# Rotating the weight rings of a decoder layer from group to group, two homes for its decay tables, and reloads paced by weight splits

## The chip, the cores and the metric

The kernel runs on one core of one Trainium2 chip. The metric is device time in microseconds of one execution; the number given for a kernel is the median of its runs. A profiled execution is shown by its span, from the first to the last instruction.

The engines are named as the profile names them: PE is TensorE (its weight loads are PEld), DVE is VectorE, ACT is ScalarE, POOL is GpSimd, and SP is the engine whose queue issues nearly all transfers. POOL's queue issues a few.

## The reference, cut to what matters

One hybrid decoder layer, batch 1, 512 tokens, model width 2048, everything in float32:

```python
h = rms_norm(x, g_mix);  z = h @ w_in            # 2048 x 7168: aq ak av | rq rk rv rg
a_out = moba_attention(rotary(norm(aq)), rotary(norm(ak)), av)      # 8 heads of 128
r = retention_chunkwise(rotary(rq), rotary(rk) * 128**-0.5, rv)     # 8 heads of 128
r = r * rsqrt(mean(r * r) + eps) * g_ret;  r_out = silu(rg) * r
x = x + concat(a_out, r_out) @ w_o               # 2048 x 2048
h2 = rms_norm(x, g_ffn)
x = x + (silu(h2 @ w_gate) * (h2 @ w_up)) @ w_down                  # 5632 wide
x = x + (p @ w_ple_proj) * sigmoid(rms_norm(x, g_ple) @ w_ple_gate + b)
```

In `retention_chunkwise` the scores of a chunk of 128 tokens are multiplied by a decay table, a power of one number per head: `decay[i, j] = g ** (i - j)` for `i >= j`, zero elsewhere. Head h has its own g, so each head needs its own table.

## The kernel before, in words

**Two parts for precision.** A float32 operand is used as a high part (a copy rounded to float32r, made by ACT) and a low part (the rest, made by DVE). `split` makes both. A product is three matmuls (`mm3`): high by high, high by low, low by high. A raw weight tile of 128 x 1024 is split by one ACT operation (`wh`, L54) and one DVE operation (`wl`, L55).

**Groups, parts, units and steps.** The large products run as groups (class `Group`). A group multiplies a 512-token operand by weights in blocks [kh, nh] of two by two, with seven products instead of eight (a scheme of Strassen's kind). The seven products are called parts, in the order 1, 5, 6, 3, 7, 2, 4. A group has four units (three in some down-projection groups), and a step is one part of one unit: 12 matmuls. So a whole group has 28 steps. Some groups run the first three parts in an order by units (`in_units`). For each step, the weight tile is added up two to three steps ahead on DVE (`add`, L83), split two steps ahead (`extract`), and multiplied (`multiply`).

**The raw tiles and their rings.** A group takes four blocks of each unit: "11", "12", "22" and "21". Each lies in a raw tile of 512 KB, in one of three rings of four tiles, with the tags `l1`, `bd` and `c`. Part 1 splits "11"; part 5 adds "12" to it, part 6 adds "22"; part 3 splits "22"; part 7 adds "22" to "12" and splits that, and then "21" is loaded into the ring of "22"; part 2 splits "21"; part 4 adds "21" to the tile of "11" and splits that. So the tile of "12" is done with at the split of part 7, that of "21" at the addition of part 4, and that of "11" at the split of part 4. As soon as a tile is done with, `load_next` loads a block of the next group into that ring:

```python
    elif p == "4":
        plus(r("11"), r("11"), r("21"))
        self.load_next("22", u)          # in add
    ...
    if p == "4":
        self.load_next("11", u)          # in extract
    elif p == "7":
        self.load_next("12", u)
```

Three groups (the first up/gate group, the last down-projection group and the first of the last gate) take sums that POOL's queue has formed ahead in DRAM (`sums`); their tiles are called by the part, "1", "5", "6" and so on, and use the same rings.

**The factors.** The other operand of a group is kept as one tile per part (`Factors`): `s_o` for w_o, `s_c` for the up/gate groups, `s_d` for the down projection. Factors are either written straight into their tile (`into`) or stored in DRAM (`spill`: a `mix`, `h` or `a` tensor) and loaded back: `back` for w_o, `reload` for the others. These reloads go through SP's queue, 512 KB to 1.5 MB each.

**Heads and slots.** The attention and retention heads run beside the projections that make their q and k. Time there is counted in slots (`tick`): a slot is six matmuls of a projection. The tables ATTEND, RETAIN, V_AT and MIXED say at which slot each piece of a head is put. For a retention head RETAIN holds: `begin`, `load` (its decay table, tile `dec`), four `scores` slots, two `normed` slots, `scaled` and `result`. `scores` multiplies the scores by the decay table (L1053) and splits the product. `normed` sums squares, takes their power on POOL (L86) and multiplies by the gate tile `sg`; `scaled` (L1089) applies the power; `result` transposes on TensorE. `mixed(i)` (at the slot MIXED[i]) makes the factors of two heads from their results: those of head groups 0 to 5 go to DRAM; for groups 6 and 7, parts 1, 5, 6 and 3 are written straight into `s_o`, and parts 7, 2 and 4 go to DRAM through the `o` tiles (four of them).

Slots 1 to 160 lie beside the projections; 161 to 176 beside p @ w_ple_proj (loop over n from 0 to 3, four slots each), whose results are copied by ACT into spare tiles (`pp`, L1192) and stored by POOL's queue; 177 to 192 beside the first eight steps of w_o's first group, two slots each (`take_over`).

**Order.** The program is written in one order, and a planner with a timing model orders each engine's instructions. `keep_in_program_order` pins some (the matmuls up to step 8 of w_o), `issue_after` puts one instruction behind another of the same engine, and `paced` makes a transfer wait until a given instruction is done. An engine, SP's queue included, runs its instructions in order. A tile of a ring or tag can't be written until its last reader is done. `lead` holds the last weight split.

Of the kernel before, what the change touches and what calls it, by code (L numbers as in the profile page):

```python
# [17 lines left out]
P = 128  # L18
T = 512
# [14 lines left out]
def layer_kernel(ctx, tc, x, xT, pT, g_mix, wqk, w_vg, qk_norm, g_ret, w_ow, g_ffn,  # L34
# [218 lines left out]
            k, n = (k - self.part) % 8, where.shape[1]  # L253
            return nc.sync.dma_start(self.tile(k // 6)[:, k % 6:k % 6 + n].bitcast(F32), where.bitcast(F32))

    def reload(tiles, where, n, wait={}, part=0):

        def go(p):
            tiles[p].load(part, where[p][:, :min(n, 6)])
            if n == 8:  # L260
                tiles[p].load(6, where[p][:, 6:])
            if n < 6 and p == "4":
                tiles[p].load(6, where[p][:, n:])
        def after(p):
            if not part:
                tiles[p] = Factors(p, 0, n != 6)
            later(wait[p], lambda: go(p)) if p in wait else go(p)
        return after
# [9 lines left out]
    class Group:  # L278
        def __init__(self, src, units, tiles, evac, order=None, after=lambda p: None, ready=lambda p, u: None, sums=None):
            self.sums = sums  # L280
            self.src, self.units, self.tiles, self.evac = src, units, tiles, evac
            self.after, self.ready = after, ready
            self.raw, self.bank, self.w, self.next = {}, {}, {}, None
            self.pinned = self.ends = self.spread = False
            self.left = {p: len(units) for p in ORDER}
            steps.extend((self, p, u) for p, u in
                         (order or [(p, u) for p in ORDER for u in range(len(units))]))

        def load(self, q, u):
            where = None  # L290
            tag = {"11": "l1", "12": "bd"}.get(q, "c")
            if self.sums:
                q = {"11": "1", "12": "5", "22": "6"}.get(q, q)
                tag = {"5": "bd", "7": "bd", "6": "c", "2": "c"}.get(q, "l1")
                where = self.sums[q][u] if q in self.sums else None
            a = SOURCE.get(q, q)
            t = rawq.tile([P, 2, T], F32, name="raw", tag=tag)
            ins = nc.sync.dma_start(t, self.src(int(a[0]) - 1, int(a[1]) - 1, self.units[u]) if where is None else where)
            if self.pinned:
                tc.keep_in_program_order(ins)  # L300
            self.raw[q, u] = t
# [8 lines left out]
        def add(self, p, u):  # L310
            r = lambda q: self.raw[q, u]
            if self.sums:
                return
            if p == "5":
                plus(r("11"), r("11"), r("12"))
            elif p == "6":
                plus(r("11"), r("11"), r("22"))
            elif p == "7":
                plus(r("12"), r("12"), r("22"))
                self.load("21", u)  # L320
            elif p == "4":
                plus(r("11"), r("11"), r("21"))
                self.load_next("22", u)

        def extract(self, p, u):
            wh = wq.tile([P, 2, T], F32R, name="wh", tag="wh")
            wl = wq.tile([P, 2, T], F32R, name="wl", tag="wl")
            with ExitStack() as queued:
                if first_parts:
                    queued.enter_context(tc.issue_after(first_parts.pop(0).ins))  # L330
                parts = split(wh, wl, self.raw[p if self.sums else SOURCE[p], u])
            lead[0] = parts[0]
            self.w[p, u] = wh, wl
            if self.sums and p in "1563":
                self.load({"1": "3", "5": "7", "6": "2", "3": "4"}[p], u)
            if self.sums and p == "2":
                self.load_next("22", u)
            if p == "4":
                self.load_next("11", u)
            elif p == "7":  # L340
                self.load_next("12", u)
            self.ready(p, u)
            return parts

# [33 lines left out]
                self.after(p)  # L378
                self.evac(self, p)

    def chained(groups):
        for a, b in zip(groups, groups[1:]):
            a.next = b
        for q in ("11", "12", "22"):
            for u in range(len(groups[0].units)):
                groups[0].load(q, u)
# [259 lines left out]

    kinds = [values(0), pairs(), values(1), gates()]
    groups = [Group(lambda kh, nh, u, j=j: w_vg[j, kh, nh, u], range(4), s_h, kinds[j]) for j in range(4)]
    for j in range(3):
        groups[j].next = groups[j + 1]  # L650
    groups[0].pinned = True
    def beside(i):

# [375 lines left out]
    def retain(qk, v, j, h):  # L1029
# [3 lines left out]
            own["qk"] = [x if isinstance(x, tuple) else parted(x) for x in (qk[j], qk[2 + j])]  # L1033

        def load():
            own["dec"] = ap.tile([P, P + T], F32, name="dec", tag="dec")
            nc.sync.dma_start(own["dec"], decay_c[h])

        def scores(kb):
            if kb == 0:  # L1040
                own["p"] = p_tiles()
                own["sg"] = rp_tile("sg", (P, NB, HD))
                nc.sync.dma_start(own["sg"], sgd[:, :, h * HD:(h + 1) * HD])
            PH, PL = own["p"]
            (qH, qL), (kH, kL) = own["qk"]
            q0 = min(kb, 2) * P
# [49 lines left out]
            nc.scalar.activation(a, tp, AF.Copy, scale=gr[:, h:h + 1])  # L1096
            return a

        return begin, load, scores, normed, scaled, result


    def back(p, pairs):
# [5 lines left out]
    def mixed(i, made):  # L1108
# [3 lines left out]
        with ExitStack() as queued:  # L1112
            for ins in lead if i < 2 * NPAIR - 1 else ():
# [7 lines left out]
              ((23, four(26, 31), four(31, 38), 44), (34, four(39, 45), four(45), 53)),  # L1121
              ((48, four(53), four(57), 70), (59, four(63, 73), four(72, 77), 81)),
              ((75, four(79), four(83), 92), (85, four(89), four(93, 103), 107)))
    RETAIN = (((104, 103, 108, 114, 118, 121), (112, 113, 116, 122, 126, 128)),
# [3 lines left out]
    MIXED = (37, 57, 83, 109, 139, 152, 179, 191)  # L1128

    def heads(i, made):  # L1130

# [15 lines left out]
                end(last, result)  # L1147
        else:
            for j, (first, at, step_s, step_n, step_x, last) in enumerate(RETAIN[i - NPAIR]):
                begin, load, scores, normed, scaled, result = retain(made, v, j, 2 * (i - NPAIR) + j)  # L1150
                plan.extend(((first, begin), (at, load), (step_x, scaled)))
                put(scores, *range(step_s, step_s + NB))
                put(normed, step_n, step_n + 1)
# [18 lines left out]
    for n in range(NS):  # L1172
        wh, wl = weights()
        accs = [acc_p.tile([P, T], F32, name="acc", tag="acc") for _ in range(NB)]
        for b in range(NB):
# [7 lines left out]
                t = ev_tile("t", 2, name="pp")  # L1183
            elif n == 1 and b < 2:
                if b == 0:
                    room = ap.tile([P, 2, T], F32, name="pp", tag="rope2")
                t = room[:, b]
            elif n:
                t = rm_tile("pp")
# [2 lines left out]
            copied = nc.scalar.activation(t, accs[b], AF.Copy)  # L1192
            copies.append(copied)
            nc.gpsimd.dma_start(ppd[b][:, n], t)
        for p in "156" if n < 3 else ():
            paced(back(p, slice(2 * n, 2 * n + 2)), copied)
    paced(back("3", slice(0, 6)), copied)
    first_parts.append(copies[4 * NS - 5])
    acc_ctx.close()

# [3 lines left out]
    def take_over(i):  # L1204

        if 0 <= i < 8:
            tick()
            tick()
        if i == 5:
            at_ctx.close()  # L1210
            pools["chainY"] = ctx.enter_context(pool("chain3", space=PSUM, side="right"))
# [17 lines left out]
    for n in range(2):  # L1229
# [1 line left out]
                            residual(n, 0, 4, lambda tb, s: x[tb * P:(tb + 1) * P, s * T:(s + 1) * T],  # L1231
                                     lambda tb, s: xd[0][tb][:, s], (1, gf, s_h2, s_c, 0)),
                            None if n else in_units(((0, 1, 2), (3,))),
                            reload(s_c, s_h2, 4, behind | {"1": 4, "3": 14, "7": 14, "2": 14, "4": 14}) if n else lambda p: None))

    def swiglu(j):
        kg = min(j // 4, 2)
# [88 lines left out]
    def gate(n):  # L1326
        def ahead(th, nh, b):
# [4 lines left out]
            get(t, tb, s)  # L1332
            if n == 1 and (tb, s) == (NB - 1, NS - 1):
                for r in range(NB):
                    both = rawq.tile([P, 2, T], F32, name="both", tag="bd")
                    coming[r, s - 1] = both[:, 0], both[:, 1]
                    get(coming[r, s - 1], r, s - 1)
            return t
# [106 lines left out]
```

## Time and profile before

| | |
|---|---|
| median of 3 runs | 2344.28 us (2343.18 to 2346.57) |
| the profiled execution | 2344.99 us, span 2343.2 us |
| mean granted TensorE clock | 0.993 |
| PE busy | 2297.7 us (98%) |
| PEld, DVE, ACT, POOL busy | 1895.8, 1917.9, 1245.0, 113.7 us |
| transfers | 520.77 MB, mean 222 GB/s |

Busy time of PE is a share of the whole span; what is left is waiting at a few places, and the profile names each by the instruction that ended the wait. "PE at L63 <- DVE pt L1053: 8.2, 1, 8.2" reads: matmuls of line 63 that write tile `at` waited for the DVE operation of line 1053 that writes `pt`, 8.2 us in total, once, at most 8.2. In the timeline a wait stands in square brackets behind the instruction that it delayed. SPq rows are issues of SP's queue: the time in them is that of issuing, not of the transfer.

### The profile page before, as it was taken

The page shows a single profiled execution, that of the slowest core. Times are in us where ns is not written, and L with a number is a line of the kernel's source. Part 1 is how long each engine was busy: PE and PEld are TensorE (multiplying, and loading weights), DVE is VectorE, ACT ScalarE, POOL GpSimd, SP SyncE. Part 2 cuts the span into 40 slices and gives each one's busy share as a digit, 9 for nine tenths or more (in the row PEclk, how much of TensorE's full clock was granted, in tenths as well). Part 3 has the DMA queues.
Part 4 walks back from the last instruction along what each step waited for, and adds up shares of the span by engine and source line. Part 5 has one row for each costly group of instructions (what it writes and reads, how often), then busy time and mean ns, then how long its engine had stood idle before and what let it go on. Part 6 is the DMA issues. An engine that isn't in the chain of part 4 may idle for free.

```text
span 2343.2 us, 29536 instructions
## 1 busy us (share of the span) xinstructions
PE 2297.7 (98%) x10445; PEld 1895.8 (81%) x10445; DVE 1917.9 (82%) x2569; ACT 1245.0 (53%) x1974; POOL 113.7 (5%) x135
## 2 busy tenths in 40 slices
PE   9999999999989998999999999999999999999999
PEld 7888887778877787888888888888888878888877
DVE  8877887776767896888988898889889877788798
ACT  8645554555674565545544554455444443447643
POOL 0002010100120000000000000000000000000000
PEclk9999999999998999999999999999999999999999
DMA  6746844556696689477557754775595776769863
GB/s 239 245 142 193 278 165 149 171 173 194 203 320 235 211 304 317 139 238 225 164 155 238 231 152 161 238 227 156 188 390 197 252 296 197 290 232 357 296 207 126
DMA packets 184420, 520.77 MB, mean 222 GB/s; under 512 B 20304, under 2 KB 33232, under 8 KB 180176
## 3 DMA queue, kind: packets, MB, share of 16 engines
q1 hardware_dynamic: 170176, 468.54, 56.3%
q0 software_dynamic: 13952, 50.34, 10.0%
q8 instruction: 82, 1.34, 0.2%
q14 instruction: 66, 0.54, 0.1%
q10 hardware_dynamic: 144, 0.01, 0.0%
HBM read 415.00 MB, written 149.95 MB: 241 GB/s over the span
## 4 chain that ended last, share of the span: by engine, by line
PE 78%; DVE 11%; DMA 7%; issue 2%; ACT 2%; POOL 0%; SPq 0%; DVEq 0%; ACTq 0%
PE Y L63 29%; PE Z L63 20%; PE X L63 18%; PE acc L63 7%; DVE wl L55 4%; DVE raw L83 3%; PE at L63 2%; PE tp L68 2%; DMA raw<-in_w_dn 1%; ACT wh L54 1%; DMA dec<-in_decay_c 1%; DMA raw<-in_w_vg 1%; DMA h<-o 1%; DMA xin<-x 1%; DVE o L55 1%
## 5 line engine op out<-in xcount | busy, mean ns | idle before, releaser
L54 ACT ACTIVATE wh<-raw 128x1024 fp32r<-128x1024 f32 (+1 forms) x740 | 783.0, 1059 | 868.0 <-PE Y L63 304.9
L55 DVE TENSOR_TENSOR wl<-raw,wh 128x1024 fp32r<-128x1024 f32 (+1 forms) x740 | 902.6, 1222 | 315.2 <-ACT wh L54 313.7
L63 PE MATMUL Y<-wh,s 128*128 128x512 f32 (+1 forms) x1704 | 538.4, 390 | 0.6 <-ACT wh L54 0.6
L83 DVE TENSOR_TENSOR raw<-raw 128x1024 f32<-128x1024 f32 x348 | 421.5, 1221 | 14.8 <-DMA raw<-in_w_dn 8.6
L63 PE MATMUL Z<-wh,s 128*128 128x512 f32 x1212 | 381.9, 389 | 0.0
L63 PEld LDWEIGHTS Y<-wh,s 128*128 128x128 f32 x1704 | 320.2, 188 | 66.7 <-ACT wh L54 1.0
L63 PE MATMUL Y<-wl,s 128*128 128x512 f32 x852 | 333.5, 391 | 0.7 <-DVE wl L55 0.7
L63 PE MATMUL X<-wh,s 128*128 128x512 f32 x1008 | 321.2, 392 | 6.7 <-ACT wh L54 6.7
L63 PEld LDWEIGHTS Z<-wh,s 128*128 128x128 f32 x1212 | 227.2, 188 | 46.1
L63 PE MATMUL Z<-wl,s 128*128 128x512 f32 (+1 forms) x606 | 238.4, 393 | 2.6 <-DVE wl L55 2.4
L63 PEld LDWEIGHTS X<-wh,s 128*128 128x128 f32 x1008 | 190.7, 189 | 46.8 <-ACT wh L54 7.4
L63 PE MATMUL X<-wl,s 128*128 128x512 f32 x504 | 198.7, 394 | 1.2 <-DVE wl L55 1.1
L63 PEld LDWEIGHTS Y<-wl,s 128*128 128x128 f32 x852 | 160.5, 188 | 34.0 <-DVE wl L55 1.1
L63 PE MATMUL Y<-wh,r 128*128 128x512 f32 x520 | 170.7, 389 | 1.1 <-ACT wh L54 1.1
L63 PE MATMUL acc<-h,wh 128*128 128x512 f32 x512 | 162.5, 399 | 0.5 <-DVE zr L1006 0.5
L63 PEld LDWEIGHTS Z<-wl,s 128*128 128x128 f32 x606 | 113.8, 188 | 27.9 <-DVE wl L55 5.0
L63 PE MATMUL Z<-wh,r 128*128 128x512 f32 x372 | 122.0, 388 | 0.0
L63 PEld LDWEIGHTS Y<-wh,r 128*128 128x128 f32 x520 | 97.4, 188 | 21.4 <-ACT wh L54 1.5
L63 PEld LDWEIGHTS X<-wl,s 128*128 128x128 f32 x504 | 95.5, 189 | 22.6 <-DVE wl L55 2.9
L63 PEld LDWEIGHTS acc<-h,wh 128*128 128x128 f32 x512 | 91.8, 190 | 16.4 <-DVE zr L1006 1.1
L63 PE MATMUL Y<-wl,r 128*128 128x512 f32 x260 | 102.0, 392 | 0.0
L63 PE MATMUL acc<-h,wl 128*128 128x512 f32 x256 | 100.7, 394 | 0.0
(245 smaller groups left out, 2842.6 us busy)
## 6 DMA issues: line engine op xcount, KB each, us to landing
raw<-in_w_gu SPq DMA_DIRECT2D x172, 512.0 KB, 5.5
raw<-in_w_dn SPq DMA_DIRECT2D x85, 512.0 KB, 6.3
a<-o SPq DMA_DIRECT2D x154, 256.0 KB, 5.0
raw<-in_w_vg SPq DMA_DIRECT2D x64, 512.0 KB, 5.6
s<-a SPq DMA_DIRECT2D x21, 1536.0 KB, 8.6
raw<-in_wqk SPq DMA_DIRECT2D x47, 512.0 KB, 4.8
raw<-in_w_ow SPq DMA_DIRECT2D x32, 512.0 KB, 5.6
xin<-x SPq DMA_DIRECT2D x60, 256.0 KB, 5.9
```

The lines of the kernel that those rows point to most:

```text
L54: return (nc.scalar.activation(H, src, AF.Copy), nc.vector.tensor_tensor(L, src, H.bitcast(F32), op=ALU.subtract))
L55: nc.vector.tensor_tensor(L, src, H.bitcast(F32), op=ALU.subtract))
L63: ins = nc.tensor.matmul(*args, **kw)
L68: ins = nc.tensor.transpose(o, a, ident)
L83: nc.vector.tensor_tensor(o, a, b, op=ALU.add)
```

## The change

Three things change. No product, split or addition is added or removed.

1. *Rings.* A group's three rings have roles that rotate: the next group's "11" goes into the ring of this group's "12" (free at part 7), its "12" into the ring of "22" (free at the addition of part 4), and its "22" into the ring of "11" (free at the split of part 4).
2. *Decay tables.* The tables of even heads lie in the tag `rope2` (free after the attention heads), those of odd heads in `dec`; their loads are put at earlier slots. The gate tile of the last head is loaded at slot 170 instead of at its first scores. mixed(6) moves from slot 179 to 172. The pp tiles of n = 1 move from `rope2` to `rope`.
3. *Reloads.* w_o's "1" and "5" are loaded in three pieces each, one piece per pp block, "5" one block behind "1"; "6" and "3" are loaded whole, ahead of steps 0 and 3 of w_o, paced by the latest weight split. The reloads of parts 3, 7, 2 and 4 of the up/gate groups' factors are paced by the latest weight split too.

```diff
-    def reload(tiles, where, n, wait={}, part=0):
+    def reload(tiles, where, n, wait={}, part=0, by=""):
         def go(p):
-            tiles[p].load(part, where[p][:, :min(n, 6)])
+            ins = tiles[p].load(part, where[p][:, :min(n, 6)])
+            if p in by:
+                paced(ins, lead[0])
...
+            self.tag = {"11": "l1", "12": "bd", "22": "c"}
...
         def load(self, q, u):
-            tag = {"11": "l1", "12": "bd"}.get(q, "c")
+            tag = self.tag[{"21": "22", "3": "11", "4": "11", "7": "12", "2": "22"}.get(q, q)]
             if self.sums:
                 q = {"11": "1", "12": "5", "22": "6"}.get(q, q)
-                tag = {"5": "bd", "7": "bd", "6": "c", "2": "c"}.get(q, "l1")
...
             elif p == "4":
                 plus(r("11"), r("11"), r("21"))
-                self.load_next("22", u)
+                self.load_next("12", u)
...
             if self.sums and p == "2":
+                self.load_next("12", u)
+            if p == "4":
                 self.load_next("22", u)
-            if p == "4":
+            elif p == "7":
                 self.load_next("11", u)
-            elif p == "7":
-                self.load_next("12", u)
...
-    def chained(groups):
+    def linked(groups):
         for a, b in zip(groups, groups[1:]):
             a.next = b
+            b.tag = {"11": a.tag["12"], "12": a.tag["22"], "22": a.tag["11"]}
+
+    def chained(groups):
+        linked(groups)
...
-    for j in range(3):
-        groups[j].next = groups[j + 1]
+    linked(groups)
...
         def load():
-            own["dec"] = ap.tile([P, P + T], F32, name="dec", tag="dec")
+            own["dec"] = ap.tile([P, P + T], F32, name="dec", tag=("rope2", "dec")[h % 2])
             nc.sync.dma_start(own["dec"], decay_c[h])
+        def load_gate():
+            own["sg"] = rp_tile("sg", (P, NB, HD))
+            nc.sync.dma_start(own["sg"], sgd[:, :, h * HD:(h + 1) * HD])
         def scores(kb):
             if kb == 0:
                 own["p"] = p_tiles()
-                own["sg"] = rp_tile("sg", (P, NB, HD))
-                nc.sync.dma_start(own["sg"], sgd[:, :, h * HD:(h + 1) * HD])
+                if "sg" not in own:
+                    load_gate()
...
-    RETAIN = (((104, 103, 108, 114, 118, 121), (112, 113, 116, 122, 126, 128)),
-              ((120, 121, 124, 135, 139, 142), (128, 129, 137, 143, 147, 149)),
-              ((142, 141, 145, 151, 155, 158), (150, 149, 153, 159, 165, 168)),
-              ((161, 163, 168, 174, 179, 184), (161, 176, 176, 182, 187, 190)))
-    MIXED = (37, 57, 83, 109, 139, 152, 179, 191)
+    RETAIN = (((104, 103, 108, 114, 118, 121), (112, 105, 116, 122, 126, 128)),
+              ((120, 114, 124, 135, 139, 142), (128, 123, 137, 143, 147, 149)),
+              ((142, 133, 145, 151, 155, 158), (150, 145, 153, 159, 165, 168)),
+              ((161, 161, 168, 174, 179, 184), (161, 162, 176, 182, 187, 190)))
+    MIXED = (37, 57, 83, 109, 139, 152, 172, 191)
...
+                if (i, j) == (2 * NPAIR - 1, 1):
+                    plan.append((170, load_gate))
...
                 if b == 0:
-                    room = ap.tile([P, 2, T], F32, name="pp", tag="rope2")
+                    room = ap.tile([P, 2, T], F32, name="pp", tag="rope")
...
-        for p in "156" if n < 3 else ():
-            paced(back(p, slice(2 * n, 2 * n + 2)), copied)
-    paced(back("3", slice(0, 6)), copied)
+        for p, k in (("1", n), ("5", n - 1)):
+            if 0 <= k < 3:
+                paced(back(p, slice(2 * k, 2 * k + 2)), copied)
...
     def take_over(i):
+        if i in (0, 3):
+            paced(back("6" if i == 0 else "3", slice(0, 6)), lead[0])
...
-  reload(s_c, s_h2, 4, behind | {"1": 4, "3": 14, "7": 14, "2": 14, "4": 14}) if n else lambda p: None))
+  reload(s_c, s_h2, 4, behind | {"1": 4, "3": 14, "7": 14, "2": 14, "4": 14}, by="3724") if n else lambda p: None))
...
-                    both = rawq.tile([P, 2, T], F32, name="both", tag="bd")
+                    both = rawq.tile([P, 2, T], F32, name="both", tag=groups[-1].tag["12"])
```

More of the change, by code (lines that the diff above doesn't have):

```diff
@@ L1097, in result @@
             return a
-        return begin, load, scores, normed, scaled, result
+        return begin, load, load_gate, scores, normed, scaled, result
     def back(p, pairs):
@@ L1149, in heads @@
             for j, (first, at, step_s, step_n, step_x, last) in enumerate(RETAIN[i - NPAIR]):
-                begin, load, scores, normed, scaled, result = retain(made, v, j, 2 * (i - NPAIR) + j)
+                begin, load, load_gate, scores, normed, scaled, result = retain(made, v, j, 2 * (i - NPAIR) + j)
+                if (i, j) == (2 * NPAIR - 1, 1):
+                    plan.append((170, load_gate))
                 plan.extend(((first, begin), (at, load), (step_x, scaled)))
```

## The prediction

> **What bounds the kernel now.** I read the page's first part, then who TensorE waited for, then the chain of waits, and last the stretches around each long wait. All stage letters below (A to D) are mine.
>
> ```profile
> span 2343.2 us, 29536 instructions
> PE 2297.7 (98%) x10445; PEld 1895.8 (81%) x10445; DVE 1917.9 (82%) x2569; ACT 1245.0 (53%) x1974; POOL 113.7 (5%) x135
> ...
> PE at L63 <- DVE pt L1053: 8.2, 1, 8.2
> PE X L63 <- ACT wh L54: 6.7, 2, 6.6
> PE tp L68 <- ACT r L1089: 4.6, 1, 4.6
> ```
>
> TensorE is busy 2297.7 of 2343.2 us, so the whole price of waiting is 45.5 us, and no change of order can win more than that plus what the matmuls lose to a low granted clock. Three single waits make 8.2 + 6.6 + 4.6 = 19.4 us of it. The diff touches what precedes all three. The chain says what each hangs on:
>
> ```profile
> 49.45 10.88 PE X L63 x48
> 661.07 0.44 PE tp L68 x4
> 685.69 17.67 DMA dec<-in_decay_c
> 704.13 1.01 PE at L63 x3
> 705.14 4.68 PE X L63 x12
> 709.82 0.36 PE at L63 x3
> 727.09 3.68 POOL rs L86
> 732.61 10.09 PE Y L63 x36
> 867.82 8.79 DMA s<-h
> 876.67 9.05 DMA raw<-in_w_gu
> 888.10 3.93 PE X L63 x12
> ```
>
> In rows of the chain the columns are start, us, what. 48 matmuls take 10.88 us at full clock, so one step of a group (12 matmuls) takes 2.72 us. **A** (at 696 us): the last retention head's decay table is on its way for 17.67 us, and the scores wait. **B** (at 727): the last head's transposes wait for a POOL power. **C** (at 880): the first up/gate group waits for its first raw weight tile.
>
> ```profile
> 676.00:696.00 20.00, 19.94 (x104) 16.76 (x102) 8.79 (x16) 13.66 (x31) 8.04 (x14) 1.00 1.00 382
> 696.00:704.20 8.20, 0.07 (x1) 0.07 (x1) 3.61 (x5) 3.28 (x9) 0.54 (x1) 0.68 1.03 413
> 704.20:710.00 5.80, 5.80 (x18) 4.75 (x19) 5.32 (x12) 2.35 (x6) 0.00 (x0) 0.57 0.84 325
> 718.00:731.20 13.20, 8.70 (x41) 6.92 (x39) 11.87 (x16) 6.36 (x16) 3.67 (x1) 0.94 0.43 140
> 880.00:887.00 7.00, 0.44 (x4) 0.20 (x2) 0.91 (x3) 1.31 (x2) 0.00 (x0) 0.73 1.03 414
> 887.00:892.00 5.00, 4.96 (x15) 3.51 (x16) 2.39 (x3) 2.39 (x3) 0.00 (x0) 0.69 1.05 412
> ```
>
> Columns: stretch, length, busy PE, PEld, DVE, ACT, POOL, granted clock, DMA share, GB/s. Before and in A and C the DMA share is 1.00 to 1.05 at 382 to 414 GB/s: both waits are transfers in a full queue. After these waits the granted clock is low (0.57, 0.69), so a wait costs more than its length. For A, 12 X matmuls take 4.68 instead of 2.72 us and three score matmuls 1.01 instead of 0.36: 8.2 + 1.96 + 0.65 = 10.8 us. For B, four transposes take 1.36 (from the row at 731.25 below) instead of 0.44 and 36 Y matmuls 10.09 instead of 8.16: 4.6 + 0.9 + 1.9 = 7.4 us. For C, 12 X matmuls take 3.93: 6.6 + 1.2 = 7.8 us.
>
> **Part 1, decay tables.** Nothing is computed differently; eight loads of 320 KB stay eight. They now alternate between the homes `rope2` and `dec` and stand 0 to 14 slots earlier; the last one moves from slot 176 to 162, behind a home that head 5 left at slot 156. The gate load of head 7 moves from 176 to 170.
>
> ```profile
> 674.17 1.34 SPq L254 DMA_DIRECT2D s<-mix  x3
> ...
> 697.76 1.90 SPq L254 DMA_DIRECT2D s<-mix  x1
> ...
> DMA to landing us min/median/max: 2.8/4.2/17.7
> ...
> s<-mix SPq DMA_DIRECT2D x9, 512.0 KB, 14.5
> ...
> s<-mix SPq DMA_DIRECT2D x1, 1536.0 KB, 14.0
> ...
> mix<-o SPq DMA_DIRECT2D x48, 256.0 KB, 4.2
> ```
>
> Columns of the last three: size, median us to landing. The row above them is of the eight decay loads (least, median, most): the last alone took 17.7 us, issued at 685.69 behind w_o's reloads, which begin at 674.17. Those are paced by the copy of slot 164; slot 162 lies ahead of it, so the table starts in a queue that is not yet full and, at the median 4.2 us, lands well before A begins at 695.9 (704.13 - 8.2). Another 10 us would be hidden too. The 8.2 us go, with their slow clock. The gate load is hidden in the same way; with no cover it would cost what it took, some us, on the same head. pp's tiles of slots 165 and 166 change to the home `rope`, whose table head group 7's rotation has finished reading by then: nothing, or one ACT copy late by a us, hidden by four accumulators. What is late next: step 0 of w_o needs its first split.
>
> ```profile
> 695.23 1.06 ACT L54 ACTIVATE wh<-raw 128x1024 fp32r<-128x1024 f32 x1 [1.15 <-PE acc L63]
> ...
> 696.32 1.23 DVE L55 TENSOR_TENSOR wl<-raw,wh 128x1024 fp32r<-128x1024 f32 x1 [1.82 <-ACT wh L54]
> ```
>
> That split waits for TensorE's own pp matmuls, and its low part ends at 697.55. A began at 695.9 and had one score block (0.36) before X: TensorE would be there at 696.3, 1.25 us early. I keep 1.6 us of the 10.8 for it: A is worth 9.2.
>
> **Part 2, mixed(6) from slot 179 to 172, and w_o's reloads.** mixed(6) is 11 operations of 256 columns on DVE and 7 on ACT. They leave the stretch from 704, where DVE works 11.87 of 13.20 us, for that of 676 to 696, where DVE has 11.2 us free and ACT 6.3: free there. Each also brings stores on SP's queue: 3 of 256 KB, now beside the reloads. w_o's reloads before the last scores shrink from nine of 512 KB and one of 1.5 MB to six of 512 KB: "6" and "3" (1.5 MB each) are paced by the weight splits of steps 1 and 4. Needed: "6" at step 6, 6 x 2.72 = 16 us plus the last head's matmuls after step 0; "3" at step 12, 33 us. The row above gives 14.0 us for 1.5 MB in a full queue, so both are hidden; if "6" took 20 us, TensorE would wait some 2 us. The wait for a split stands at SP's head; behind it are w_o's later raw tiles, residual tiles and stores. Since that split leads TensorE by a step or two, it holds them by about one step, 2.7 us, less than the slack of any of them (below).
>
> **B** does not go by itself. Between the start of step 0 and the last transposes TensorE has six steps, 16.3 us, and the head's own matmuls; DVE in that time has splits, additions and the head's work, which keep it nearly full, and the power comes behind them.
>
> ```profile
> L86 POOL TENSOR_TENSOR rs<-ms,neghalf x8: 1400/1421/3672, 582.1 to 727.1; 128x4 f32<-128x4 f32 x8
> ...
> 383.89 0.63 PE L68 MATMUL tp<-ident,pt 128*128 128x128 f32 x4 [2.13 <-DVE pt L966]
> 731.25 1.36 PE L68 MATMUL tp<-ident,r 128*128 128x128 f32 x4 [4.55 <-ACT r L1089]
> ...
> 382.00:387.00 5.00, 3.11 (x13) 2.67 (x14) 3.04 (x7) 1.18 (x3) 0.00 (x0) 0.79 0.39 141
> ```
>
> The power takes 1.42 us in the median of eight and 3.67 here, beside the full DVE. Ends: nothing gained, or all 7.4. mixed(6)'s departure takes about 11 x 0.31 = 3.4 us from DVE, an estimate from a quarter of the 1.23 us of the 1024-column operation at 696.32; but during A's stall DVE did 3.61 us of work while TensorE stood, and that lead is gone. The two cancel, so I stay near the low end and take 2, about what the power would save on a freer DVE (3.67 - 1.42). If the wait stays between 2 and 3 us, it costs some slow clock too, as the 2.13 us wait at 383.89 does (granted 0.79 in its stretch). The Trainium skill ("TensorE: Matmul & The Clock Gate", Part 1) puts the throttle behind an idle window of about 3.4 us: by that rule a shorter rest of B would be free of slow clock and the estimate 1 us lower; the 2.13 us row speaks against the rule here.
>
> **Part 3, the rings.** Loads, sizes and moments of issue stay; only which data goes into which freed ring. A group's "12" ring comes free at step p7, eight steps before the "11" ring at p4. Before, the next group's "11", needed first, waited for the latest ring: from its issue behind step 24's split to its own split at step 28 less two there are about 4 steps, 10.9 us. Now "11" has 12 steps, "12" and "22" at least 8 in whole groups, 21.8 us; in the first up/gate group, whose order takes 1, 5, 6 early, "12" has 6 and "22" 4. The slow raw tile at 876.67 took 9.05 us in a full queue, so whole groups are safe.
>
> ```profile
> 845.05 0.38 SPq L298 DMA_DIRECT2D raw<-sgu  x1
> ...
> 867.82 0.81 SPq L254 DMA_DIRECT2D s<-h  x2
> ...
> 876.67 0.33 SPq L298 DMA_DIRECT2D raw<-in_w_gu  x1
> ```
>
> At C, "11" takes the place of the load at 845.05 and lands long before 880. The tile that is now issued at 876.67 is "22" (kept sum "6"), first split ahead of step 4, 880.3 + 4 x 2.72 = 891 less 2; with the 9.05 us of before it lands at 885.7. Besides, four reloads of 1 MB (parts 3, 7, 2, 4; two, by their place, are the row at 867.82) are now paced by splits and leave that stretch: at 412 GB/s 4.2 MB are 10 us of queue. They are needed from step 12 on, 33 us in, and take about 9 us (8.79 at 867.82). What is late next is DVE's residual work: I keep 0.5 us, C is worth 7.3.
>
> **D**, small waits where the down projection's groups begin:
>
> ```profile
> ACT wh L54 <- DMA raw<-in_w_dn: 19.4, 7, 5.1
> ...
> PE X L63 <- DVE wl L55: 1.7, 3, 0.6
> PE Z L63 <- DVE wl L55: 0.7, 1, 0.7
> ```
>
> Between 1700 and 1960 us these are 2.4 us on TensorE, behind an ACT that waits 19.4 us for raw tiles, which come earlier now. I take 2. Groups inside the eleven up/gate groups show no TensorE wait: nothing to win. The paced reloads add waits at SP's head; raw loads queue behind them, but have 8 steps of slack.
>
> **Sum.** 9.2 + 2 + 7.3 + 2 = 20.5 us. The profiled execution took 2344.99 us (span 2343.2), 0.7 above the median of 2344.28: 2344.99 - 20.5 - 0.7 = 2323.8, so 2324.
>
> **Rivals.** *The pp copies take A's place* (15%). mixed(6) now takes three of the four `o` tiles just before pp's last four copies, which need them too; three copies on ACT wait for stores. mix stores land in 4.2 us in the median, reloads in the full queue in 14.5. Splits done at 694, stores at 698 (fine) or 708 (X1's bank, copied last, opens after that): then A gives about 1, the sum is 12.3, 2332. For it: DMA share 1.00. Against: 1.5 MB less in flight.
>
> *C only moves on* (12%): "22" or its reloads come late, TensorE waits some 5 us at step 4 or 12. The sum is 15 to 16: 2329.
>
> *It does not do what it says* (8%): SP's order is a planner's; if it leaves the last table behind a wait on SP, A stays, B too, and C is half: 2341.
>
> *Slower* (9%): the same `o` wait, but on ACT's head. ACT runs in order; the blocked copy also holds the last head's PH splits and w_o's splits. B, C and D give 11.3; to end 4.7 us above now, step 0 would have to begin 16 us after today's 704.9, that is a store 27 us under way. Price then 2350. Against: no transfer in A's rows is longer than 17.7.
>
> **How the numbers follow.** The forecast has 56%, its own range 2316 (A, B and C whole: 10.8 + 7.4 + 7.8 + 2) to 2329. The other cases on the fast side reach 2332; with some reordering noise the range is 2315 to 2336. Beyond it lie the last two rivals and a little more. 0.2% is 4.7 us, about what a measurement of this kernel can tell from no change: faster 0.56 + 0.15 + 0.12, same 0.08, slower 0.09.
>
> **What would show it.** Right: no TensorE wait on DVE pt L1053; the last decay load landing before 680; the first w_gu tile issued near 845 on the old clock, and X starting without a wait on ACT wh. Wrong: a wait of X1 on the pp copies; ACT waiting for mix stores; Z or Y waiting for s tiles of w_o or the first up/gate group; the transposes of L1089 still waiting over 4 us.

## The result, and the profile after

| kernel | median | ratio to the kernel before (95%) | profiled execution |
|---|---|---|---|
| before | 2343.73 us (2342.5 to 2346.57, 4 runs) | 1 | span 2343.2 us |
| after | 2326.4 us (2323.78 to 2328.7, 4 runs) | 0.9924 (0.9907 to 0.9941) | 2328.7 us, span 2326.9 us |

The change makes the kernel 17.3 us faster. The forecast was 2324. The sum of its terms was 20.5 us, the spans differ by 16.3, and the terms came out otherwise than forecast: C and D gave more, A and B together gave 3.1 of the 11.2 forecast for them. The page's first part after the change:

```profile
span 2326.9 us, 29623 instructions
...
PE 2294.7 (99%) x10445; PEld 1895.8 (81%) x10445; DVE 1917.9 (82%) x2569; ACT 1245.1 (54%) x1974; POOL 106.2 (5%) x135
```

Whom TensorE waited for, after (total us, times, longest us):

```profile
PE acc L63 <- ACT pp L1204: 4.8, 1, 4.8
PE tp L68 <- ACT r L1099: 4.3, 1, 4.3
...
PE tp L68 <- DVE ms L631: 3.3, 1, 3.3
PE Y L63 <- ACT wh L54: 2.9, 3, 1.1
```

Of the three long waits of before, A's (8.2) and C's (6.6) are gone and B's (4.6) is still 4.3, now from line 1099. At the head stands a new one: the third product (p @ w_ple_proj) waits 4.8 us for an ACT copy of its own results.

To see where time went, both traces are cut at the same instructions: the first retention head's power on POOL, and runs of 48 Z matmuls on the chain. The stretches that hold A and B together, C, and D, in the kernel before; the last rows are one 20 us slice of D and the sum over all of D's slices:

```profile
582.07:750.85 168.78, 155.60 (x765) 131.15 (x764) 120.02 (x203) 104.87 (x240) 27.62 (x29) 0.95 0.71 240
...
750.85:922.87 172.02, 163.21 (x738) 132.99 (x737) 140.26 (x202) 101.13 (x168) 2.14 (x3) 0.98 0.81 288
...
1900.00:1920.00 20.00, 18.10 (x76) 13.70 (x75) 16.49 (x17) 7.37 (x8) 0.00 (x0) 1.00 0.91 355
...
sum 236.25, PE 232.88 PEld 190.11 DVE 195.41 ACT 104.43 POOL 0.00; mean PE 25.88 PEld 21.12 DVE 21.71 ACT 11.60 POOL 0.00
```

The same stretches after:

```profile
581.84:747.48 165.64, 156.08 (x765) 131.40 (x764) 120.23 (x203) 105.03 (x240) 27.64 (x29) 0.96 0.73 244
...
747.48:910.12 162.64, 161.24 (x738) 132.20 (x737) 140.07 (x202) 100.61 (x168) 2.13 (x3) 1.00 0.82 294
...
sum 232.04, PE 231.04 PEld 190.63 DVE 195.18 ACT 104.78 POOL 0.00; mean PE 25.67 PEld 21.18 DVE 21.69 ACT 11.64 POOL 0.00
```

The matmuls in A+B and in C are as many as before (765 and 738). A+B shrinks by 3.14 us (forecast 11.2), C by 9.38 (forecast 7.3), D by 4.21 (forecast 2); the rest of the span grows by 0.4, and the sum is the 16.3. In C the idle time (length less busy PE) falls from 8.81 to 1.40 and the busy time by 1.97, with the granted clock up from 0.98 to 1.00. In A+B the idle time falls only from 13.18 to 9.56, busy PE grows by 0.48, and the clock is 0.96 against 0.95.

What replaced A's wait, in the timeline after (start, us, engine, line; in brackets the wait ahead and who ended it):

```profile
685.91 0.58 ACT L1204 ACTIVATE pp<-acc 128x512 f32<-128x512 f32 x1
...
686.84 0.42 DVE L80 TENSOR_TENSOR t<-r,t 128x256 f32<-128x256 f32 x1
...
686.90 0.55 POOL L1206 DMA_DIRECT2D pp<-pp  x1 [1.55 <-ACT pp L1204]
...
695.60 0.69 DVE L55 TENSOR_TENSOR PL<-pt,PH 128x512 fp32r<-128x512 f32 x1 [0.76 <-ACT PH L54]
696.21 0.75 DVE L80 TENSOR_TENSOR t<-r,t 128x256 f32<-128x256 f32 x2
...
697.93 1.06 ACT L1204 ACTIVATE pp<-acc 128x512 f32<-128x512 f32 x2
698.56 0.79 PE L63 MATMUL acc<-wh 128*128 128x512 f32 x1 [4.76 <-ACT pp L1204]
...
700.37 1.32 ACT L1204 ACTIVATE pp<-acc 128x512 f32<-128x512 f32 x2 [0.43 <-DMA mix<-o]
```

mixed(6) sums and subtracts in two scratch tiles with the tag `t` (two buffers), and the copies `pp` of the third product's slots 171 and 172 lie in the same two. At slot 172 mixed(6) stands between these two copies. So the copy at 685.91 fills one `t` tile and its store is issued at 686.90; mixed(6) has one `t` tile left and makes its first two sums in it; its last two need the other tile, so they need that store to be done (the trace has its landing at 693.70), and then they stand on DVE behind the last head's work (695.60), until 696.21. The second copy goes into the tile of the first two sums, which the last two still read, so it comes behind them, as the first of the pair at 697.93. It opens the accumulator that TensorE has waited for since 693.8.

The edge of B, on DVE and POOL after:

```profile
718.89 0.41 DVE L83 TENSOR_TENSOR r<-r,at 128x256 f32<-128x256 f32 x1
719.22 1.22 DVE L83 TENSOR_TENSOR raw<-raw 128x1024 f32<-128x1024 f32 x1
...
721.83 1.22 DVE L83 TENSOR_TENSOR raw<-raw 128x1024 f32<-128x1024 f32 x1
722.97 0.15 DVE L1090 TENSOR_SCALAR ms<-ms 128x4 f32<-128x4 f32 x1
...
723.21 3.68 POOL L86 TENSOR_TENSOR rs<-ms,neghalf 128x4 f32<-128x4 f32 x1 [19.15 <-DVE ms L1090]
723.64 2.35 DVE L55 TENSOR_TENSOR wl<-raw,wh 128x1024 fp32r<-128x1024 f32 x2
...
727.37 1.35 PE L68 MATMUL tp<-ident,r 128*128 128x128 f32 x4 [4.29 <-ACT r L1099]
```

The mean-square step `ms` of the last head follows additions of later steps' weights (`raw`), the power follows `ms`, and it takes 3.68 us beside two weight subtractions on DVE.

### The profile page after: what moved, and what is told of

Read it like the earlier page. It is cut to its first block, busy times and chain, and to the rows that moved or that the text cites. A ratio compares the mean times of both kernels' runs of the same rounds, so it can differ in the third digit from the quotient of the medians.

```text
span 2326.9 us, 29623 instructions
## 1 busy us (share of the span) xinstructions
PE 2294.7 (99%) x10445; PEld 1895.8 (81%) x10445; DVE 1917.9 (82%) x2569; ACT 1245.1 (54%) x1974; POOL 106.2 (5%) x135
## 3 DMA queue, kind: packets, MB, share of 16 engines
q8 instruction: 82, 1.34, 0.2%
## 4 chain that ended last, share of the span: by engine, by line
PE 86%; DVE 7%; DMA 3%; issue 2%; ACT 1%; POOL 0%; SPq 0%; DVEq 0%; ACTq 0%
PE Y L63 32%; PE Z L63 22%; PE X L63 20%; PE acc L63 8%; PE at L63 2%; DVE wl L55 2%; PE tp L68 2%; DVE raw L83 2%; DMA h<-o 1%; ACT wh L54 1%; DMA raw<-in_w_dn 0%; DMA raw<-in_w_ow 0%; DVE o L55 0%; DMA sn<-in_rope_c 0%; DVE e L83 0%
## 5 line engine op out<-in xcount | busy, mean ns | idle before, releaser
L63 PEld LDWEIGHTS acc<-h,wh 128*128 128x128 f32 x512 | 92.1, 190 | 16.3 <-DVE zr L1012 1.1
```

The costliest lines, as they stand in the source:

```text
L63: ins = nc.tensor.matmul(*args, **kw)
```

## Experiments

All were run in five rounds beside the kernel before, whose medians in the three sets were 2345.31, 2344.43 and 2343.95 us. Ratios are to those. "Stage" below is the length of the same three stretches as above.

**mixed(6) back to slot 179.**

```diff
-    MIXED = (37, 57, 83, 109, 139, 152, 172, 191)
+    MIXED = (37, 57, 83, 109, 139, 152, 179, 191)
```

> The changed kernel with mixed(6) back at slot 179; all else stays. Theory 'scratch tiles': in the changed kernel mixed(6) at 172 holds a scratch tile t that a pp copy needs, and TensorE waits 4.8 us for that copy, with slow clock behind it (some 2.5 us). Without it no wait on the pp copies, X of w_o starts near 697, and the whole is 4 to 7 us faster than the changed kernel (2326.4), so 2319 to 2322; the wait at the last transposes stays or grows by up to 3 us. Rival 'start of w_o': the first weight split of w_o bounds the start of X anyway, and DVE gets 3.4 us more work before the last transposes: within 2 us of 2326, or slower.

Measured: 2324.67 us, ratio 0.9909 (0.9895 to 0.9922). The 4.76 us wait is gone (X waits 1.00 us for a last copy); stage A+B is 160.81 us (583.84 to 744.65), 4.8 under the changed kernel's. So mixed(6) at slot 172 made that wait. The total is another matter: it is 1.7 us under 2326.4, which is what the rival expected, and the intervals overlap. The reason stands in its rows: with the mixing back among the last head's work, two shorter waits appear in B's place.

```profile
712.58 0.39 PE L63 MATMUL at<-v,PL 128*128 128x256 f32 x1 [2.40 <-DVE PL L55]
...
725.47 1.21 PE L68 MATMUL tp<-ident,r 128*128 128x128 f32 x4 [2.29 <-ACT r L1099]
```

So slot 172 cost more at its new place than it gave. Whether it relieved DVE later can't be read from this pair, since TensorE also comes there some 4 us later in the changed kernel; slots 171 and 179 with the mean-square step first, below, show that it does.

**The rings alone** (the kernel before with part 3 of the prediction):

```diff
+            b.tag = {"11": a.tag["12"], "12": a.tag["22"], "22": a.tag["11"]}
...
+                self.load_next("12", u)      # at the addition of part 4
...
+                self.load_next("22", u)      # at the split of part 4
+            elif p == "7":
+                self.load_next("11", u)
```

> The kernel before with the rotating rings alone (decay tables, mixed(6) and reloads as before). Theory 'rings': the wait of X for its first raw tile at 880 us (6.6 us and slow clock) and the small waits at the starts of w_o's second and the down projection's groups go: 12 to 13 us less, 2331. Rival 'queue': the paced reloads emptied the queue there; without them the first tiles are still late by 3 us or more at 880, and 5 to 7 us less, 2337 to 2339. Both: the 8.2 us wait for the decay table stays.

Measured: 2331.73 us, ratio 0.9944 (0.993 to 0.9958). The wait of C is gone without any pacing, and stage D is 232.24 us, all of the gain that the whole change has there. A's wait (shorter by 2 us) and B's stay:

```profile
PE at L63 <- DVE pt L1057: 6.1, 1, 6.1
PE tp L68 <- ACT r L1093: 4.8, 1, 4.8
```

Stage C is 164.26 us, 7.76 less than before.

**The paced reloads of the up/gate factors alone:**

```diff
+            if p in by:
+                paced(ins, lead[0])
...
+  reload(s_c, s_h2, 4, behind | {...}, by="3724")
```

> The kernel before with the pacing of the up/gate factors' reloads (parts 3, 7, 2, 4) alone. Theory 'rings': the first raw tile is still issued near 877 us and needs at least 5 us to land; the wait at 880 shrinks by 0 to 3.5 us, 2340 to 2344. Rival 'queue': that wait goes, 7 to 8 us less, 2336.

Measured: 2338.04 us, ratio 0.9967 (0.9955 to 0.998). Stage C is 167.53 us, 4.49 less, although no ring was changed; D is 236.44, as before. The theory, that only rings take C's wait, missed (it had 2340 to 2344); the rival was nearer. What is left of C's wait on ACT:

```profile
PE X L63 <- ACT wh L54: 1.3, 1, 1.3
```

So C's wait had two removers in the change. The rings alone take it all; the pacing alone takes 5.3 of its 6.6 us. Their two gains (7.76 and 4.49) do not add: together they give 9.38.

**The decay tables alone** (homes, slots, gate load, `pp` tiles; mixed(6) at 179, reloads as before):

```diff
+            own["dec"] = ap.tile([P, P + T], F32, name="dec", tag=("rope2", "dec")[h % 2])
...
-              ((161, 163, ...), (161, 176, 176, 182, 187, 190)))
+              ((161, 161, ...), (161, 162, 176, 182, 187, 190)))
```

> The kernel before with the decay tables' two homes, their early loads, the last head's early gate load and pp's move to the home rope; mixed(6) at 179, reloads and rings as before. Theory 'scratch tiles': nothing holds the pp copies, the 8.2 us wait goes with its slow clock: 8 to 10 us less, 2334 to 2336. Rival 'full queue': nine reloads of 512 KB and one of 1.5 MB ahead of step 0 delay another transfer there (gate tile, pp stores or w_o's first raw tiles), and less than 5 us is won, 2339 or more.

Measured: 2338.11 us, ratio 0.997 (0.9959 to 0.9982), between the two expectations. A's wait is gone (the first X matmul waits 1.00 us instead), and B's wait grows:

```profile
PE tp L68 <- ACT r L1093: 7.4, 1, 7.4
PE X L63 <- ACT wh L54: 4.7, 1, 4.7
```

Stage A+B is 162.24 us, 6.54 under before, twice the 3.14 that the whole change has in it. TensorE comes to the last head's transposes 9.6 us earlier than before (717.1 against 726.7), but the power starts only 6.7 us earlier (720.36 against 727.09), so part of A's 8.2 us returns as B. C's wait is 4.7 us here instead of 6.6, with rings and pacing as before: some of it hangs on what goes ahead.

**mixed(6) at 174, behind both copies that use `t`:**

```diff
+    MIXED = (37, 57, 83, 109, 139, 152, 174, 191)
```

> The changed kernel with the seventh entry of MIXED at 174 in place of 172, nothing else. Theory of the scratch tiles: at 174 the second product of the scores' third section has left its scratch tile before the mixing asks for it, so the 4.76 us wait of the third product on a copy goes, and the last head's mixing is still far ahead of the output projection: 2320 to 2323 us, 3 to 6 us under the changed kernel. Rival, the ring of the small scaled tiles: the last copies of the third product wait for the stores of the mixed tiles, and X of the output projection waits 2 to 5 us: about 2325 us, no gain on the changed kernel.

Measured: 2333.12 us, ratio 0.9955 (0.9942 to 0.9967): slower than the changed kernel's 0.9924 (0.9907 to 0.9941), which neither side expected. The 4.76 us wait is gone here too, although mixed(6) still stands ahead of the third product's last three copies: the scratch tiles were its cause. But the ring `o` now holds the third product's last copies:

```profile
704.10 1.57 SPq L228 DMA_DIRECT2D mix<-o  x3
...
706.50 0.60 ACT L1204 ACTIVATE pp<-acc 128x512 f32<-128x512 f32 x1 [1.88 <-DMA mix<-o]
707.48 0.60 ACT L1204 ACTIVATE pp<-acc 128x512 f32<-128x512 f32 x1 [0.39 <-DMA mix<-o]
...
708.13 0.79 PE L63 MATMUL X<-wh,s 128*128 128x512 f32 x1 [11.98 <-ACT pp L1204]
```

mixed(6) at slot 174 stands between the copies of slots 173 and 174, and the `o` tiles go in that order: one copy, three tiles of mixed(6), then three copies, of which the last two wait for mixed(6)'s stores. These stores are issued only at 704.10, since DVE had the last head's scores and w_o's splits in front of mixed(6). The prediction's first rival was this mechanism, put at slot 172, where it costs 0.43 us on ACT. Two slots later it costs 12.

**The mean-square step ahead of the additions** (mixed(6) at 172 as changed; the additions of w_o's later steps are ordered behind `ms` of the last head):

```diff
-            nc.vector.tensor_scalar(ms, ms, 1.0 / HD, EPS, op0=ALU.mult, op1=ALU.add)
+            ins = nc.vector.tensor_scalar(ms, ms, 1.0 / HD, EPS, op0=ALU.mult, op1=ALU.add)
+            if h == 2 * NPAIR - 1:
+                last_p.append(ins)
```

> The changed kernel, with one ordering edge more: the later additions of partial sums on VectorE are made to stand behind the last head's mean-square step, so that the chain normalisation, power, scaling isn't delayed by them. Theory that the additions ahead of it on VectorE set that chain: the 4.29 us wait of the last head's transposes and the 1.9 us of slow clock behind it go: 2319 to 2321 us. Rival, that the power's own 3.69 us on GpSimd and the copies bound it: a gain under 2 us, 2325 us or more. The 4.76 us wait of the scores' product stays in both.

Measured: 2324.58 us, ratio 0.991 (0.9895 to 0.9925). B's wait is gone altogether, its power takes 1.44 us:

```profile
717.40 0.17 DVE L1090 TENSOR_SCALAR ms<-ms 128x4 f32<-128x4 f32 x1 [0.23 <-ACT pt L1087]
...
717.65 1.44 POOL L86 TENSOR_TENSOR rs<-ms,neghalf 128x4 f32<-128x4 f32 x1 [12.91 <-DVE ms L1090]
...
718.11 4.62 DVE L83 TENSOR_TENSOR raw<-raw 128x1024 f32<-128x1024 f32 x4
```

Stage A+B is 159.87 us, 5.8 under the changed kernel's. That is the mechanism, shown: DVE's order set B. It did so in two ways that this run doesn't separate: `ms` comes earlier, and the power behind it is 2.24 us shorter. The total falls between the two expectations: in this profile D is 1.1 us longer (233.13 us; the run with the old reloads, below, has 233.02 without the edge, so it is not the edge's doing) and the first retention head comes 0.9 us later. Its interval overlaps that of the changed kernel's first set, so the total alone proves little.

**Both: slot 179 and the mean-square step first.**

> The changed kernel with the seventh entry of MIXED at 179 and the same ordering edge for the mean-square step. If both losses are separate: 2318 to 2320 us, the 4.76 us wait and the 4.29 us wait both gone. If the mixing at 179 and the additions compete for VectorE in the same stretch, one wait of 2 to 4 us stays before the output projection's second group: 2322 to 2325 us.

Measured: 2321.14 us, ratio 0.9898 (0.9885 to 0.9912), between the two expectations. Both long waits are gone; the longest that stay in the stretch are 1.34 and 1.27 us. Stage A+B has 156.25 us: 4.57 are idle, and the granted clock is 1.00.

```profile
582.88:739.13 156.25, 151.68 (x765) 127.71 (x764) 118.47 (x203) 104.29 (x240) 25.39 (x29) 1.00 0.75 242
```

**Slot 174 and the mean-square step first.**

> The changed kernel with the seventh entry of MIXED at 174 and the same ordering edge for the mean-square step. If both losses are separate and the mixing at 174 leaves VectorE free earlier than at 179: 2315 to 2319 us, the least of the four. If the edge only moves VectorE's queue on: the gain of the entry at 174 alone, 2320 to 2323 us.

Measured: 2330.44 us, ratio 0.9939 (0.9927 to 0.9952). Both expectations missed, for the reason of the other run at 174: X waits 12.0 us again. B's wait is gone here too.

**w_o's reloads back in their old pattern** (all else as changed):

```diff
-        for p, k in (("1", n), ("5", n - 1)):
-            if 0 <= k < 3:
-                paced(back(p, slice(2 * k, 2 * k + 2)), copied)
+        for p in "156" if n < 3 else ():
+            paced(back(p, slice(2 * n, 2 * n + 2)), copied)
+    paced(back("3", slice(0, 6)), copied)
...
-        if i in (0, 3):
-            paced(back("6" if i == 0 else "3", slice(0, 6)), lead[0])
```

> The changed kernel with the output projection's factor reloads (parts 1, 5, 6, 3) issued as in the kernel before, all inside the loop of the third product; everything else of the change stays. Theory that this part of the change is free: within 2 us of the changed kernel, and no new wait over 1 us before the output projection's second group. Rival, that the early reloads crowd SP's queue and push the last decay table or the raw tiles of w_o back: a wait of 2 to 5 us before the output projection, and 2 to 5 us more.

Measured: 2328.51 us, ratio 0.9938 (0.9925 to 0.995); the changed kernel in the same set had 2330.61, ratio 0.9938. The waits are the same two, 4.75 and 4.30 us. This part of the change is worth nothing that can be measured, once the tables load early.

**Slots 177 and 171, both with the mean-square step first.**

> The changed kernel with the seventh entry of MIXED at 177 (the first slot after the third product's last copy) and the ordering edge for the last head's mean-square step. Theory that 172 loses by the scratch tiles and 174 by the ring of scaled tiles: at 177 both are behind, so it runs as with 179: ratio to the kernel before about 0.990, no wait of over 1.5 us between 690 and 760 us. Rival, that the mixing just ahead of the output projection holds ACT and VectorE when its first tiles are split: a wait of 2 to 4 us at X, 2323 to 2325 us.

> The changed kernel with the seventh entry of MIXED at 171 (ahead of both copies of the third product that use the scratch tiles) and the same ordering edge. By the theory of the scratch tiles the mixing now takes both tiles first and the two copies wait for it instead: a wait of the third product on a copy of 1 to 5 us stays, 2321 to 2325 us. If the mixing gets through before the copies are due, no wait is left there: ratio 0.989 to 0.990.

Measured: 2319.44 us, ratio 0.9896 (0.9883 to 0.991) at 177; 2318.32 us, ratio 0.989 (0.9875 to 0.9906) at 171. Slot 177 is the first behind all copies, slot 171 the last ahead of the two that share `t`. At 177 the theory held: no wait over 1.35 us in the stretch. At 171 the wait that I had put first does not come. The whole mixing runs through on a DVE that has room, and the copies of slots 171 to 173 follow at once; X still waits 1.79 us for a later copy:

```profile
682.04 0.42 DVE L80 TENSOR_TENSOR t<-r 128x256 f32<-128x256 f32 x1
...
686.57 1.55 ACT L1206 ACTIVATE pp<-acc 128x512 f32<-128x512 f32 x3
...
686.86 0.76 DVE L55 TENSOR_TENSOR o<-r,o 128x256 fp32r<-128x256 f32 x2
```

Its stage A+B is the shortest, 13.98 us under before, with 3.40 idle. That is 1.45 us less than with slot 179, where the first matmul on `PL` waits 1.27 us; here that wait is gone, so moving the mixing ahead did relieve DVE:

```profile
580.56:735.36 154.80, 151.40 (x765) 127.55 (x764) 118.57 (x203) 103.78 (x240) 25.47 (x29) 1.00 0.74 244
```

**The changed kernel again**, beside these three.

> The changed kernel as it is, once more, so that the three others are compared with it on one chip: ratio to the kernel before 0.992 to 0.993, the 4.76 us and the 4.29 us waits as in its first profile.

Measured: 2330.61 us, ratio 0.9938 (0.9926 to 0.9951), with the same two waits (4.76 and 4.29). In this set the version with slot 171 is 12.3 us faster, and the intervals are apart. It beats both kernels; so does that with 177, and the runs don't tell these two from each other.

## Why the prediction was right and wrong

The total, 2324 against 2326.4, came out near because errors of both signs met: A and B together gave 8.1 us less than forecast, C and D 4.3 more. That is luck, and not a sum that held.

**A, forecast 9.2.** The step on the decay table held. The eight loads after the change landed in

```profile
DMA to landing us min/median/max: 2.9/4.2/7.0
```

against 17.7 for the last one before, and no matmul waits for `pt` of the last head. What failed is the sentence on mixed(6), "free there". It counted DVE's and ACT's spare time between 676 and 696 and looked at one shared ring, `o`. It did not list the other tiles that mixed(6) takes: its two `t` tiles are those of two copies of the third product. A wait of 4.76 us with its slow clock followed, and X began only 1.8 us earlier than before (703.17 against 704.94). The signs that were to show a wrong step did so: a wait on the `pp` copies, though of the accumulators and not of X, and transposes that still wait over 4 us. Slots 171 and 177 (with the edge at `ms`) and slot 179 (without it) show no such wait, only 1.79, 1.30 and 1.00 us of X: one slot earlier or five later the move was nearly free there.

**B, forecast 2, measured nothing.** The transposes waited 4.29 instead of 4.55 us, and the power took 3.68 instead of 3.67. The low end that the prediction named was the right value. Its reason, that DVE's 3.4 us of mixing and A's lost lead cancel, was only half of it: what counts is how many additions stand ahead of `ms` and what stands beside the power, and the edge that puts `ms` ahead of the additions removed the wait. The run with the tables alone shows that A and B are one path: part of what is won at A without moving the power comes back at B.

**C, forecast 7.3, measured 9.38.** The mechanism is right, and there were two, each close to enough alone. Three small things were left out of the sum. In the same stretch, three short waits of w_o's later groups (0.81, 0.73, 0.68 us) became 0.83, 0.16 and 0.41; and "0.5 us for the residual work" wasn't needed, since X of the first up/gate group now starts with no wait at all; and busy PE fell by 1.97 us, where 1.2 was counted.

**D, forecast 2, measured 4.21.** The waits were counted, but not what a wait costs beyond its length. Idle time fell by 2.37 us, about what was forecast, and busy PE by 1.84 more. The slice from 1900 to 1920 of before shows why: four short waits made 1.9 us idle, and 76 matmuls ran instead of the 90 of a full slice. At 20/90 us each the 14 missing ones are 3.1 us. The granted clock there is 1.00, so it isn't the clock. Two of the four in the timeline before:

```profile
1907.14 0.73 PE L63 MATMUL X<-wh,s 128*128 128x512 f32 x2 [0.15 <-ACT wh L54]
1908.39 0.50 PE L63 MATMUL X<-wl,s 128*128 128x512 f32 x1 [0.52 <-DVE wl L55]
1908.73 0.63 PE L63 MATMUL X<-wh,s 128*128 128x512 f32 x2
```

A row of one matmul is 0.39 us long, but at full pace the next one starts 0.23 us after it (10.88 us for 48), so 0.16 us of each wait is counted as busy. And the matmul behind a wait takes 0.50 us and the next starts 0.34 behind it, 0.11 late. That makes 0.27 us beyond the length shown, whatever the length: 1.1 us for the four, and with the 1.9 us the 3.0 that are missing. D had seven waits before and has two after, so 1.4 of the 1.84 us are of this kind; the rest is not accounted for.

**The rivals.** "The pp copies take A's place" came true in kind (the copies hold TensorE) and not by the ring it named, and at 172 with about half of its price, 4.76 us. "C only moves on", "it does not do what it says" and "slower" are excluded by the rows above. The sum of "it does not do what it says" left out D: with D's 2 us it would have been about 2339.

## What to carry to other kernels

Before work is moved to a place where engines have time, list every tile that it takes there, with tag and buffers, and who else takes that tag nearby: an order between two users of a small ring can cost more than the whole move wins, and a shift by one or two slots can turn 0 into 12 us. A short wait costs more than its length even at full clock: in the one slice examined here each cost 0.27 us more than the profile shows, so count the waits in a sum as well as their length. When two waits lie on one path, price the second again with the first removed.

## What the hardware showed that was not expected

**The clock gate.** Which waits are followed by a low granted clock (it is the last figure but two) can be read from stretches that start where a wait ended. After waits of 2.08 us (slot 174) and 4.29 us (the changed kernel), each ahead of the last head's transposes:

```profile
731.98:737.00 5.02, 5.02 (x15) 3.78 (x16) 2.89 (x8) 2.76 (x7) 0.00 (x0) 0.66 0.00 0
```

```profile
727.37:732.37 5.00, 5.00 (x14) 3.80 (x15) 2.83 (x8) 3.53 (x10) 0.00 (x0) 0.50 0.00 0
```

After a wait of 1.79 us at X (slot 171):

```profile
697.96:703.00 5.04, 5.04 (x25) 4.29 (x26) 5.04 (x8) 3.20 (x7) 1.68 (x3) 1.00 0.98 396
```

These three look like a limit near 2 us, but the length of the wait alone doesn't decide. The transposes at 384 us, which the change does not touch, wait 2.13 us before the change and 2.12 after it (the first row is of before, the second of after). And with the paced reloads alone, waits of 1.29 and 0.53 us at X are followed by a low clock (the third):

```profile
383.89:388.89 5.00, 5.00 (x19) 4.17 (x20) 1.97 (x6) 1.73 (x5) 0.00 (x0) 0.66 0.01 5
```

```profile
384.02:389.02 5.00, 5.00 (x27) 4.30 (x28) 2.93 (x9) 2.70 (x6) 0.00 (x0) 1.00 0.09 34
```

```profile
880.79:885.79 5.00, 4.47 (x12) 3.22 (x13) 4.42 (x6) 3.99 (x9) 0.00 (x0) 0.67 0.96 347
```

So waits of 2.29 us (slot 179) and more were all followed by a low clock in these runs, and shorter ones sometimes; what decides there stays open. The prediction held the wait at 383.89 against a limit of 3.4 us; the same wait in the changed kernel would have spoken for it. The Trainium skill ("TensorE: Matmul & The Clock Gate", Part 1) names an idle window of about 3.4 us; the waits of 2.08 and 2.13 us lie below it and were followed by a low clock all the same.

**The power beside DVE.** It takes 1.40 to 1.45 us in most places, 2.54 us with one low-half subtraction of a weight tile right behind the gate multiplication on DVE (slots 174 and 179 for mixed(6)) and 3.68 us with two. In each of the long ones it ends 0.90 us after those subtractions (725.99 and 726.89 after the change: 723.64 + 2.35 and 723.21 + 3.68). The Trainium skill ("SBUF — State Buffer", "Who interferes with whom") says that a DVE instruction with two SBUF inputs contends with a GpSimd instruction that reads SBUF; these rows agree. But not every such instruction holds the power. In the run with the mean-square step first, additions with two SBUF inputs stood in the same place (718.11), and the power took 1.44 us and ended 0.90 us after the gate multiplication. Nor is it additions against subtractions: after the change, the power at 638.95 takes 1.40 us with a subtraction (`PL`, 639.38) right behind the gate multiplication, and the one at 672.16 takes 2.52 us and ends 0.90 us after an addition (`zr`, 673.09 + 0.68). What tells them apart stays open.
